# First modulation turned later, input-projection weights in three pairs, filter sums beside their values, one more modulation group in the projection

## The chip, the core and the metric

The kernel runs on one core of one Trainium2 chip. The metric is the device time of one execution in microseconds (us). The core has a matrix engine (TensorE, PE in the profile), a vector engine (VectorE, DVE), a scalar engine (ScalarE, ACT), GpSimd (POOL) and a sync engine (SyncE, SP), which here only issues DMAs. Each engine works through its own list of instructions in the order in which they were written into it; engines wait for each other by semaphores.

## The reference

Two layers of a hybrid backbone over 1024 latent tokens and 256 context tokens, model width 1024, float32 throughout.

```python
for i in range(DEPTH):                                   # layer 0 is even, layer 1 odd and last
    sh1, sc1, g1, sh2, sc2, g2 = ada_mod(c, ada_w[i], ada_b[i])          # silu(c) @ w + b, six groups of 1024
    u_lat = modulate(rms_norm(h_lat, norm1_g[i]), sh1, sc1)              # h*(1+scale)+shift
    u_ctx = modulate(rms_norm(h_ctx, norm1_g[i]), csh1, csc1)            # same with the context's condition
    if even: y = u @ w_in -> first 512 channels: 2-D FFT groups; other 1536: short conv, Hyena long conv; @ w_out
    else:    y_lat = neighbourhood attention (latent rows, all context keys) @ w_out
    h = h + g1 * y
    h = h + g2 * swiglu(modulate(rms_norm(h, norm2_g[i]), sh2, sc2), w_gate, w_up, w_down)
return rms_norm(h_lat, final_g)
```

The long convolution of layer 0 is done in the frequency domain. Its filters come from a small sine MLP over time; each filter is normalised over time: `h = h / sum(|h|)`. A "modulation" is one group of 1024 columns of `ada_mod`, for both conditions (latent and context); layer 0 has six, numbered m = 0 to 5 (0 shift, 1 scale, 2 gate of the first half, 3 to 5 the same of the second).

## The kernel before, in words

Products are done with operands cut in two: `split` writes a rounded high part (`wh`, ACT cast, line 349) and a low part (`wl`, DVE subtraction, line 351), and a product is three matmuls: high by high, low by high, high by low (`mm`, line 345). Loads are issued by SP (`ld`, line 330) or by POOL (`ldr`, line 336). Tiles come from pools: `S4` (1024 floats a partition), `S2`, `G`, `T` (512), and `W(tag)` for weights with rings by tag: `wh` and `wl` have two places each, `ws`, the staging of a weight before its split, four. A new tile of a ring waits until the tile that held its place is no longer used, and what stands behind it in the same engine's list waits with it.

The work is written by Python generators. `run` draws from them in turns, and that order, placed once more by a scheduler when the program is built, sets each engine's list. Latent tokens are two pieces of 512 columns, context is one of 256. The stages of layer 0 and their places in the profiled execution:

- start (to about 115 us): row norms of `x` and `ctx` (`first_norm`), the filters' MLP (`filter_mlp`), and the first two modulations (`ada_first`: m = 1, then m = 0). `ada_first` loads eight blocks of 128 rows of weight per modulation through POOL into S4, forms two PSUM rows of 2x512, copies them on ACT (line 505), turns them into columns by eight small matmuls, and adds the bias on DVE (lines 512, 515). `first_norm` then turns the normed rows and applies the columns.
- `in_proj` (about 115 to 540 us): 16 blocks of 128 output columns of `w_in`; for each, `weights` loads 128x1024 into `ws` and splits it into a `wh`/`wl` pair, 72 matmuls follow. Block i then draws from fillers by a count per block: `long` (for both orders o: `filter_raw` makes the filter values, `spectrum_l` their spectrum by DFT matmuls), `filt` (the same for the context length, `spectrum_c`), `ada` (modulation groups, below), and `four` and `conv` of the context. From block 4 a block ends in `short_conv` (ACT line 1009, DVE lines 1010 to 1013).
- the latent long convolution with `inverse_last` (to about 780 us), the output projection `out_proj` (evictions on DVE at line 1657, squares for the second norm at lines 577 and 582, the second norm and its transforms by `wino_first`, lines 1724 to 1727; to about 882 us), and the SwiGLU. Layer 1 is the rest, 882 to 2990 us.

`filter_sum("l", o, raw)` forms sum |h|: for four blocks of values, two absolute values on ACT, a maximum and an addition on DVE (lines 780, 782), then ten small matmuls with ones. `spectrum_l` starts it and draws from it in the last two of its four classes.

`ada_group(l, m, conds, where)` makes later modulations on DVE alone: for each of eight column blocks it multiplies a weight tile with the broadcast condition and sums (line 552), four half-tiles per step; `late_groups(ms)` runs several. In `in_proj` the group is m = 2; m = 3 and 4 are drawn in `inverse_last` and `out_proj`.

Of the kernel before, what the change touches and what calls it, by code (L numbers as in the profile page):

```python
# [258 lines left out]
class Builder:  # L259
    def __init__(self, ctx, tc, a, out, taps=None, stop=None):  # L260
# [15 lines left out]
        self.mj = 0  # L276
# [86 lines left out]
    def pair3(self):  # L363

        self.p3 = (getattr(self, "p3", 0) + 1) % 4
# [121 lines left out]
    def ada_first(self):  # L487
# [6 lines left out]
        for m in (1, 0):  # L494
            ps = [self.PP(), self.PP()]
            for kb in range(KB):
                w = self.S4()
                self.ldr(w, a["ada_k"][m, kb])
                for j in (0, 1):
                    self.mm(ps[j][0:2, :], cond[:, 2 * kb:2 * kb + 2], w[:, j * 512:(j + 1) * 512], kb == 0, kb == KB - 1)  # L500
                yield
            col = self.PS()
            for j in (0, 1):
                row = self.G()
                nc.scalar.copy(row[0:2, :], ps[j][0:2, :])
# [21 lines left out]
    def ada_group(self, l, m, conds, where):  # L527
# [13 lines left out]
        ready = [load(m * 8)] if where == "s2" else []  # L541
        for nb in range(m * 8, m * 8 + 8):
            if where != "s2" or nb < m * 8 + 7:
                ready.append(load(nb + len(ready)))
# [17 lines left out]
    def late_groups(self, ms):  # L562

        self.load_cond(wide=False)
        for m in ms:
            yield from self.ada_group(0, m, (0, 1), "s2")
# [314 lines left out]
    def spectrum_l(self, o, raw):  # L881
# [4 lines left out]
        tot = self.filter_sum("l", o, raw)  # L886
# [59 lines left out]
        for i in classes:  # L946
            cls, eo = i % 2, i // 2
            kept = []
            for p in (0, 1):
# [3 lines left out]
                for k in (0, 1):  # L953
# [41 lines left out]
        for _ in tot:  # L995
            pass
# [19 lines left out]
    def in_proj(self, u, norm, fill, four, conv):  # L1016
# [16 lines left out]
        def filled(i):  # L1033
# [3 lines left out]
            if i > 4:  # L1037
# [14 lines left out]
        pairs = [self.weights(a["w_in"][nb]) for nb in (0, 1)]  # L1052
# [20 lines left out]
        for i, nb in enumerate(order[2:], 2):  # L1073
            wh, wl = self.weights(a["w_in"][nb])
# [1352 lines left out]
    def run(self):  # L2427
# [24 lines left out]
        for _ in range(4):  # L2452
# [4 lines left out]
        long = (x for o in (0, 1) for g in (self.filter_raw("l", raws["l"], (o,)), self.spectrum_l(o, raws["l"][o]))  # L2457
                for x in g)
        ada = self.late_groups((2,))
# [17 lines left out]
        self.in_proj(u, ng, ((long, (4, 4, 4, 4, 4, 4, 5, 5, 1)), (filt, (0,) * 7 + (2,)), (ada, (0,) * 8 + (1,))), fc, cc)  # L2477
# [5 lines left out]
        late = self.late_groups((3, 4))  # L2483
# [286 lines left out]
```

## Time and profile before

| what | value |
|---|---|
| median of three runs | 2985.84 us (2981.18 to 2989.96) |
| the profiled execution | 2991.98 us, its span 2990.1 us |
| mean granted TensorE clock of it | 0.968 |
| PE busy | 2808.6 us, 94% of the span |
| DVE, ACT, POOL busy | 2069.3, 1328.2, 542.7 us |
| PE busy, start 0 to 115 us | 82.69 of 115 us |
| PE busy, `in_proj` 115 to 540 us | 349.76 of 425 us |
| PE busy, 540 to 780 us | 221.59 of 240 us |
| PE busy, output projection 780 to 882 us | 91.84 of 102 us |
| PE busy, 882 to 2990 us | 2062.70 of 2108 us |

In lines of the profile L349 is line 349 of the kernel, `x4` a count, and a bracket at the end of a line is the engine's idle time just before the work and what ended it: `[7.88 <-DVE s L782]` is 7.88 us of waiting for an `s` tile that DVE wrote at line 782. A float32 matmul is two records. In a table of windows each engine's busy time stands with its count of instructions, then the granted clock, the share of the DMA engines and GB/s.

### The profile page before, as it was taken

How to read it: one execution, taken by the hardware profiler on the slowest of the kernel's cores; microseconds unless marked ns; L12 is line 12 of the kernel's file. 1: busy time of each engine (PE TensorE's matmuls, PEld its weight loads, DVE VectorE, ACT ScalarE, POOL GpSimd, SP SyncE). 2: the span in 40 equal slices, each digit the busy share in tenths (PEclk: the TensorE clock that was granted, in tenths of full speed). 3: DMA queues.
4: the chain of work that ended last, by engine and by line, in shares of the span. 5: the costliest groups of instructions: out<-in, count | busy, mean ns of one | idle time of the engine just before them, and what ended most of it. 6: DMA issues, size and time to landing. Idle time of an engine off the chain costs nothing. (4 is left out here: it accounts for less than half of the span.)

```text
span 2990.1 us, 43785 instructions
## 1 busy us (share of the span) xinstructions
PE 2808.6 (94%) x15570; PEld 2349.1 (79%) x15570; DVE 2069.3 (69%) x3643; ACT 1328.2 (44%) x2274; POOL 542.7 (18%) x867
## 2 busy tenths in 40 slices
PE   5888769989989999999999999999999999999998
PEld 1767558768879888888888988888887788888886
DVE  2575758777787688887678535777777987664545
ACT  3342422543355433333346434777765533333433
POOL 1021113523101122222110001323321022112000
PEclk8889879999999999999999999999999999999999
DMA  6135424666556555656897434778776276534663
GB/s 251 63 131 159 150 76 143 200 219 219 183 192 197 190 198 195 206 208 239 308 313 245 157 129 127 183 184 190 195 224 208 101 248 222 176 110 172 223 196 127
DMA packets 301673, 557.36 MB, mean 186 GB/s; under 512 B 82440, under 2 KB 128714, under 8 KB 301454
## 3 DMA queue, kind: packets, MB, share of 16 engines
q1 hardware_dynamic: 239502, 371.53, 39.8%
q0 software_dynamic: 59648, 178.83, 17.1%
q10 hardware_dynamic: 2304, 4.20, 0.4%
q8 instruction: 123, 2.02, 0.3%
q14 instruction: 96, 0.79, 0.1%
HBM read 407.10 MB, written 119.80 MB: 176 GB/s over the span
## 5 line engine op out<-in xcount | busy, mean ns | idle before, releaser
L1850 PE MATMUL ps<-s,s 128*128 128x512 f32 x1976 | 489.1, 390 | 1.6 <-ACT g L1855 1.6
L1850 PEld LDWEIGHTS ps<-s,s 128*128 128x128 f32 x1976 | 371.8, 188 | 80.1 <-ACT g L1855 2.5
L345 PE MATMUL ps<-s,wh 128*128 128x256 f32 (+1 forms) x1768 | 410.6, 336 | 18.7 <-ACT wh L349 10.0
L345 PEld LDWEIGHTS ps<-s,wh 128*128 128x128 f32 x1768 | 303.9, 196 | 54.4 <-ACT wh L349 10.6
L351 DVE TENSOR_TENSOR wl<-ws,wh 128x1024 fp32r<-128x1024 f32 (+1 forms) x141 | 167.9, 1191 | 181.9 <-ACT wh L349 179.0
L349 ACT CAST wh<-ws 128x1024 fp32r<-128x1024 f32 (+1 forms) x141 | 144.6, 1025 | 303.5 <-PE ps L345 194.9
L345 PE MATMUL ps<-s,wl 128*128 128x256 f32 (+1 forms) x884 | 272.2, 334 | 0.8 <-DVE wl L351 0.8
L345 PE MATMUL pq<-s,wh 128*128 128x512 f32 (+1 forms) x856 | 261.4, 385 | 4.0 <-DVE s L2596 2.6
L2023 PE MATMUL ps<-s,s 128*128 128x512 f32 (+1 forms) x1000 | 259.5, 383 | 3.1 <-DVE s L351 3.0
L349 ACT CAST s<-s 128x1024 fp32r<-128x1024 f32 (+2 forms) x192 | 172.4, 926 | 191.6 <-DMA s<-d 165.8
L345 PE MATMUL ps<-s,s 128*128 128x65 f16 (+4 forms) x2737 | 232.1, 238 | 21.8 <-ACT s L349 7.0
L349 ACT CAST s<-t 128x512 fp32r<-128x512 f32 (+2 forms) x238 | 134.3, 581 | 216.6 <-PE ps L1850 70.6
L351 DVE TENSOR_TENSOR s<-s,s 128x1024 fp32r<-128x1024 f32 (+2 forms) x170 | 190.9, 1154 | 50.5 <-ACT s L349 50.3
L2023 PEld LDWEIGHTS ps<-s,s 128*128 128x128 f32 x1000 | 184.6, 188 | 41.0 <-DVE s L351 4.4
L351 DVE TENSOR_TENSOR s<-t,s 128x512 fp32r<-128x512 f32 (+2 forms) x238 | 151.6, 651 | 68.4 <-ACT s L349 41.2
L1850 PE MATMUL ps<-s,wh 128*128 128x512 f32 x616 | 191.2, 390 | 0.0
L345 PEld LDWEIGHTS ps<-s,wl 128*128 128x128 f32 x884 | 170.1, 195 | 17.6 <-DVE wl L351 1.2
L345 PEld LDWEIGHTS pq<-s,wh 128*128 128x128 f32 x856 | 155.9, 191 | 32.2 <-DVE s L2596 2.7
L345 PE MATMUL pq<-s,wl 128*128 128x512 f32 (+1 forms) x428 | 163.0, 384 | 0.0
L345 PEld LDWEIGHTS ps<-s,s 128*128 128x128 f32 (+1 forms) x817 | 126.6, 195 | 34.2 <-ACT s L349 8.0
L2023 PE MATMUL ps<-s 128*128 128x512 f32 (+1 forms) x500 | 150.7, 385 | 0.0
L336 POOL DMA_DIRECT2D d<-s x154 | 83.4, 542 | 360.2 <-DVE s L1657 120.1
(479 smaller groups left out, 5588.5 us busy)
## 6 DMA issues: line engine op xcount, KB each, us to landing
s<-d SPq DMA_DIRECT2D x283, 256.0 KB, 3.8
s<-in_down SPq DMA_DIRECT2D x150, 256.0 KB, 4.2
d<-s POOLq DMA_DIRECT2D x138, 256.0 KB, 3.4
s<-in_ada_w POOLq DMA_DIRECT2D x56, 512.0 KB, 4.8
d<-tk POOLq DMA_DIRECT2D x98, 256.0 KB, 4.1
ws<-in_up SPq DMA_DIRECT2D x44, 512.0 KB, 3.8
d<-g POOLq DMA_DIRECT2D x86, 256.0 KB, 3.1
ws<-in_gate SPq DMA_DIRECT2D x42, 512.0 KB, 3.7
```

The costliest lines, as they stand in the source:

```text
L336: self.last_ldr = self.nc.gpsimd.dma_start(out, in_).ins
L345: self.nc.tensor.matmul(o, l, r, start=st, stop=sp)
L349: self.last_hi = nc.scalar.copy(hi, src).ins
L351: self.last_lo = eng.tensor_tensor(lo, src, hi.bitcast(F32), SUB).ins
L1850: nc.tensor.matmul(ps, x[:, sl], y, start=first and j == 0 and x is wh and y is xh, stop=j == 3 and x is wl, skip_group_check=True)
L2023: m = nc.tensor.matmul(acc[j][:, c0:c1], x[:, sl], y[:, xs], start=first and k == 0, stop=last and k == 2, skip_group_check=True)
```

## The change

Four things change.

1. `ada_first`: the columns of m = 1 are no longer turned when its rows are done but while m = 0 is under way (at its fifth block), and the row copies go to DVE.
2. `in_proj` takes its weights by `weights3`: every third pair goes into two places of the `ws` ring, the others into `wh` and `wl` as before. The counter `p3`, which a later stage (the SwiGLU of `pair3`) also uses, starts at 0 once, so that stage begins at another place of its own cycle.
3. `filter_sum("l")` is drawn beside `filter_raw`, at its steps k = 3, 5, 7 and so on; what is left of it, the small matmuls among it, is drawn at one place of `spectrum_l`.
4. Modulation m = 3 moves from the later stages into `in_proj`: `ada` takes (2, 3) and is drawn once a block from block 3 and twice from block 13; only m = 4 stays for later. Its weight tiles go as one load of 512 KB into the `ws` ring, where two loads of 256 KB went into S2. `long` is drawn 4 times a block and 2 from block 8, and `four` starts at block 8 where it was block 5.

```diff
-            if where == "s2":
-                st = [self.S2(), self.S2()]
-                for j in (0, 1):
-                    self.ld(st[j], a["ada_w"][l, nb, :, j * 512:(j + 1) * 512])
-                return st
+            if where == "ws":
+                t = self.W("ws", "ws")
+                self.ld(t, a["ada_w"][l, nb])
+                return [t[:, :512], t[:, 512:]]
...
+    def weights3(self, src):
+
+        self.p3 = (self.p3 + 1) % 3
+        st = self.W("ws", "ws")
+        tags = ("ws", "ws") if self.p3 == 0 else ("wh", "wl")
+        hi, lo = self.pair2(tags)
+        self.ld(st, src)
+        self.split(st, hi, lo)
+        return hi, lo
...
-        for m in (1, 0):
-            ps = [self.PP(), self.PP()]
-            for kb in range(KB):
-                w = self.S4()
-                self.ldr(w, a["ada_k"][m, kb])
-                for j in (0, 1):
-                    self.mm(ps[j][0:2, :], cond[:, 2 * kb:2 * kb + 2], w[:, j * 512:(j + 1) * 512], kb == 0, kb == KB - 1)
-                yield
+
+        def columns(m, ps):
             col = self.PS()
             for j in (0, 1):
                 row = self.G()
-                nc.scalar.copy(row[0:2, :], ps[j][0:2, :])
+                nc.vector.tensor_copy(row[0:2, :], ps[j][0:2, :])
...
+        ps = {}
+        for m in (1, 0):
+            ps[m] = [self.PP(), self.PP()]
+            for kb in range(KB):
+                w = self.S4()
+                self.ldr(w, a["ada_k"][m, kb])
+                for j in (0, 1):
+                    self.mm(ps[m][j][0:2, :], cond[:, 2 * kb:2 * kb + 2], w[:, j * 512:(j + 1) * 512], kb == 0, kb == KB - 1)
+                if m == 0 and kb == 4:
+                    columns(1, ps[1])
+                yield
+        columns(0, ps[0])
...
-    def spectrum_l(self, o, raw):
+    def spectrum_l(self, o, raw, tot):
...
-        tot = self.filter_sum("l", o, raw)
...
-                    if i >= 2:
-                        next(tot, None)
-                        if i == 3 and p == 0:
-                            for _ in tot:
-                                pass
+                    if i == 2 and p == 0 and k == 1:
+                        for _ in tot:
+                            pass
...
-            if i > 4:
+            if i > 7:
                 next(four, None)
...
-            wh, wl = self.weights(a["w_in"][nb])
+            wh, wl = self.weights3(a["w_in"][nb])
...
+        def filters():
+            for o in (0, 1):
+                tot = self.filter_sum("l", o, raws["l"][o])
+                for k, _ in enumerate(self.filter_raw("l", raws["l"], (o,))):
+                    if k > 2 and k % 2:
+                        next(tot)
+                    yield
+                yield from self.spectrum_l(o, raws["l"][o], tot)
+
+        long = filters()
+        ada = self.late_groups((2, 3))
...
-        self.in_proj(u, ng, ((long, (4, 4, 4, 4, 4, 4, 5, 5, 1)), (filt, (0,) * 7 + (2,)), (ada, (0,) * 8 + (1,))), fc, cc)
+        self.in_proj(u, ng, ((long, (4, 4, 4, 4, 4, 4, 4, 4, 2)), (filt, (0,) * 7 + (2,)), (ada, (0, 0, 0) + (1,) * 10 + (2,))), fc, cc)
...
-        late = self.late_groups((3, 4))
+        late = self.late_groups((4,))
```

How this moves instructions is shown at three places; in these rows the name before the arrow is written, those behind it are read, and the number behind a name tells tiles apart. Line numbers of the changed kernel are up to 20 higher than those of the kernel before.

First DVE's list in the start stage, around the end of the filters' MLP. Before:

```order
L701 TENSOR_SCALAR s_51_176<-s_51_176 128x640
L703 SCALAR_TENSOR_TENSOR s_48_169<-s_51_176,s_48_169 128x640 x3
L704 TENSOR_SCALAR s_48_169<-s_48_169 128x640
L715 TENSOR_TENSOR s_52_184<-s_48_169,s_52_184 64x512
L717 TENSOR_TENSOR s_53_185<-s_48_169,s_53_185 64x512
L715 TENSOR_TENSOR s_54_190<-s_48_169,s_54_190 64x128
L717 TENSOR_TENSOR s_55_191<-s_48_169,s_55_191 64x128
L512 TENSOR_TENSOR c_97<-ps_218,c_101 128x8
```

and in the changed kernel:

```order
L717 TENSOR_SCALAR s_51_176<-s_51_176 128x640
L351 TENSOR_TENSOR wl_961<-ws_959,wh_960 128x1024
L719 SCALAR_TENSOR_TENSOR s_48_169<-s_51_176,s_48_169 128x640 x3
L720 TENSOR_SCALAR s_48_169<-s_48_169 128x640
L731 TENSOR_TENSOR s_52_184<-s_48_169,s_52_184 64x512
L733 TENSOR_TENSOR s_53_185<-s_48_169,s_53_185 64x512
L731 TENSOR_TENSOR s_54_190<-s_48_169,s_54_190 64x128
L733 TENSOR_TENSOR s_55_191<-s_48_169,s_55_191 64x128
L509 COPY g_241<-ps_151 2x512
L509 COPY g_247<-ps_152 2x512
```

The split of a third weight pair, `wl_961`, now stands inside the MLP, and the two row copies behind its last line; PE's small matmuls that turn m = 1 read `g_241` and `g_247`, and PE's list has the first two matmuls of m = 0 ahead of them now.

Second DVE's list near the end of `in_proj`, where the weights of block 14 (counted from 0) are split. Before, the low half (`wl_4005`) is made ahead of the short convolution of block 13 (its lines 1010 follow it):

```order
L826 COPY t_3771<-s_956_3625 128x512
L1097 TENSOR_TENSOR s_966_3648<-t_3649 128x256
L1098 TENSOR_TENSOR s_966_3648<-t_3649 128x256
L827 TENSOR_TENSOR t_3771<-s_956_3625,s_958_3630 1x512
L828 TENSOR_SCALAR t_3771<-t_3771 1x512
L351 TENSOR_TENSOR wl_4005<-ws_4003,wh_4004 128x1024
L1010 SCALAR_TENSOR_TENSOR s_976_3741<-ps_3666,c_317,s_976_3741 128x255
L1010 SCALAR_TENSOR_TENSOR s_977_3745<-ps_3667,c_317,s_977_3745 128x511
```

and in the changed kernel, where block 14 is one of the third pairs, it (`wl_3845`) stands behind that short convolution and behind two modulation steps (line 568 is the line 552 of before):

```order
L568 ISA ws_3796,ah_3813<-ws_3796,s_470_1584,c_101 128x512
L568 ISA ah_3813 128x1
L1105 TENSOR_TENSOR t_3833<-s_991_3758,s_992_3762 128x512
L850 SCALAR_TENSOR_TENSOR t_3942<-s_995_3773,c_95,t_3784 128x512
L1544 TENSOR_TENSOR s_1015_3816<-ps_3631,t_3817 128x2x64
L1547 TENSOR_TENSOR s_1015_3816<-ps_3631,t_3817 128x63
L1548 TENSOR_TENSOR s_1015_3816<-ps_3631,t_3817 128x64
L568 ISA ws_3796,c_97<-ws_3796,s_471_1585,ah_3813 128x512
L568 ISA c_97 128x1
L1108 TENSOR_TENSOR s_1018_3832<-t_3833 128x256
L1109 TENSOR_TENSOR s_1018_3832<-t_3833 128x256
L351 TENSOR_TENSOR wl_3845<-ws_3843,wh_3844 128x1024
```

From the first of the short convolution's lines that can only run when block 13's matmuls are done, 38 rows of DVE stand ahead of this split, 16 of them (eight pairs) of modulation steps.

Third DVE's list at the end of the output projection, its evictions (line 1657, 1668 in the changed kernel) and the second norm's transforms. Before:

```order
L1724 SCALAR_TENSOR_TENSOR s_1825_7291<-s_1649_6370,c_97,t_7041 128x512
L1724 SCALAR_TENSOR_TENSOR s_1832_7331<-s_1651_6376,c_97,t_7041 128x512
L1724 SCALAR_TENSOR_TENSOR s_1836_7365<-s_1649_6370,c_97,t_7041 128x512
L1657 SCALAR_TENSOR_TENSOR s_1787_7087<-ps_7222,c_97,s_1787_7087 128x512
L582 TENSOR_TENSOR tk_7129<-tk_7129,tk_7168 128x512
L1657 SCALAR_TENSOR_TENSOR s_1788_7089<-ps_7262,c_97,s_1788_7089 128x512
L1657 SCALAR_TENSOR_TENSOR s_1789_7091<-ps_7302,c_97,s_1789_7091 128x512
L1727 SCALAR_TENSOR_TENSOR s_1798_7133<-s_1797_7131,c_97,s_1798_7133 128x512
L1727 SCALAR_TENSOR_TENSOR s_1805_7173<-s_1804_7171,c_97,s_1805_7173 128x512
```

and in the changed kernel:

```order
L1668 SCALAR_TENSOR_TENSOR s_1763_7039<-ps_7174,c_97,s_1763_7039 128x512
L598 TENSOR_TENSOR tk_7081<-tk_7081,tk_7120 128x512
L351 TENSOR_TENSOR wl_7170<-ws_7168,wh_7169 128x1024
L1735 SCALAR_TENSOR_TENSOR s_1794_7203<-s_1674_6421,c_97,t_6993 128x512
L1738 SCALAR_TENSOR_TENSOR s_1774_7085<-s_1773_7083,c_97,s_1774_7085 128x512
L1738 SCALAR_TENSOR_TENSOR s_1781_7125<-s_1780_7123,c_97,s_1781_7125 128x512
L598 TENSOR_TENSOR tk_7081<-tk_7081,tk_7160 128x512
L1738 SCALAR_TENSOR_TENSOR s_1788_7165<-s_1787_7163,c_97,s_1788_7165 128x512
L1668 SCALAR_TENSOR_TENSOR s_1764_7041<-ps_7214,c_97,s_1764_7041 128x512
L351 TENSOR_TENSOR wl_7210<-ws_7208,wh_7209 128x1024
```

Before, seven transforms of one kind and then seven of the other stand in a clump between evictions; now they are spread, one to three between two evictions. No modulation step is left in this stage's list: m = 4 takes the places that m = 3 had in `inverse_last`, and the eight steps of m = 4 that stood in the first half of `out_proj` are gone from it.

More of the change, by code (lines that the diff above doesn't have):

```diff
@@ L275, in __init__ @@
         self.k = self.mk = self.pk = 0
-        self.mj = 0
+        self.mj = self.p3 = 0
         self.held = False
@@ L363, in pair3 @@
     def pair3(self):
-        self.p3 = (getattr(self, "p3", 0) + 1) % 4
+        self.p3 = (self.p3 + 1) % 4
         tags = ("ws", "ws") if self.p3 % 2 == 0 else ("wh", "wl")
@@ L539, in load @@
             return [t[:, :512], t[:, 512:]]
-        ready = [load(m * 8)] if where == "s2" else []
+        ready = [load(m * 8)] if where == "ws" else []
         for nb in range(m * 8, m * 8 + 8):
-            if where != "s2" or nb < m * 8 + 7:
+            if where != "ws" or nb < m * 8 + 7:
                 ready.append(load(nb + len(ready)))
@@ L565, in late_groups @@
         for m in ms:
-            yield from self.ada_group(0, m, (0, 1), "s2")
+            yield from self.ada_group(0, m, (0, 1), "ws")
     def ada_col(self, l, pc, m, b):
@@ L994, in spectrum_l @@
                 yield
-        for _ in tot:
-            pass
     def short_conv(self, acc, hb):
@@ L1050, in kept @@
             return t
-        pairs = [self.weights(a["w_in"][nb]) for nb in (0, 1)]
+        pairs = [self.weights3(a["w_in"][nb]) for nb in (0, 1)]
         p01 = [{}, {}]
@@ L2456, in run @@
         next(ng)
-        long = (x for o in (0, 1) for g in (self.filter_raw("l", raws["l"], (o,)), self.spectrum_l(o, raws["l"][o]))
-                for x in g)
-        ada = self.late_groups((2,))
+        def filters():
[8 more added lines that the diff above has]
+        ada = self.late_groups((2, 3))
         filt = (x for o in (0, 1) for g in (self.filter_raw("c", raws["c"], (o,)), self.spectrum_c(o, raws["c"][o]))
```

## The prediction

> **What bounds the kernel now.** I read the page first: the span, the shares of the engines, and PE's slices.
>
> ```profile
> span 2990.1 us, 43785 instructions
> PE 2808.6 (94%) x15570; PEld 2349.1 (79%) x15570; DVE 2069.3 (69%) x3643; ACT 1328.2 (44%) x2274; POOL 542.7 (18%) x867
> PE   5888769989989999999999999999999999999998
> PEclk8889879999999999999999999999999999999999
> ```
>
> PE is the bound, and what it lacks lies in the first seven slices of 75 us; the change touches nothing behind 882 us. So only PE's idle time up to there can be won. The windows by stage give how much that is, and how full DVE is at the places that the change moves work to and from.
>
> ```profile
> core 0: us, PE busy (x) PEld busy (x) DVE busy (x) ACT busy (x) POOL busy (x), PEclk, DMA share, GB/s
> 0.00:115.00 115.00, 82.69 (x328) 46.58 (x328) 43.43 (x78) 50.24 (x82) 14.75 (x33) 0.90 0.46 166
> 115.00:540.00 425.00, 349.76 (x1646) 281.03 (x1647) 275.54 (x575) 138.43 (x266) 76.84 (x105) 0.88 0.41 132
> 780.00:882.00 102.00, 91.84 (x452) 77.67 (x451) 77.79 (x154) 42.09 (x68) 8.64 (x17) 0.93 0.58 204
> ...
> 380.00:400.00 20.00, 4.26 (x20) 3.08 (x18) 17.11 (x45) 9.39 (x18) 1.57 (x3) 0.68 0.30 92
> 460.00:480.00 20.00, 20.00 (x107) 17.13 (x106) 19.41 (x39) 4.09 (x6) 8.09 (x7) 1.00 0.60 196
> 480.00:500.00 20.00, 20.00 (x101) 16.86 (x100) 16.52 (x33) 6.57 (x12) 4.60 (x5) 1.00 0.36 119
> 500.00:520.00 20.00, 17.88 (x91) 15.03 (x91) 19.78 (x41) 7.42 (x13) 7.11 (x9) 0.83 0.56 165
> 840.00:860.00 20.00, 16.29 (x63) 12.64 (x63) 18.66 (x34) 14.36 (x24) 3.08 (x6) 0.91 0.60 213
> 860.00:880.00 20.00, 13.55 (x64) 12.10 (x62) 16.24 (x23) 10.04 (x15) 1.23 (x3) 0.74 0.52 182
> ```
>
> PE is idle for 75.2 us of `in_proj`, 32.3 of the start and 10.2 of the output projection. DVE is free for a third of `in_proj` as a whole, but from 460 to 520 it is busy for 55.7 of 60 us: modulation steps put there have no room.
>
> Then the waits up to 420 us, and PE's own rows at the stalls.
>
> ```profile
> ACT wh L349 <- PE ps L345: 72.7, 9, 18.4
> DVE wl L351 <- ACT wh L349: 58.9, 9, 10.5
> PE ps L345 <- DVE s L782: 12.0, 2, 7.9
> ```
>
> ```profile
> 190.85 0.55 PE L345 MATMUL ps<-c,s 128*128 128x1 f32 x2 [7.88 <-DVE s L782]
> ...
> 256.77 0.50 PE L345 MATMUL ps<-s,s 128*128 128x512 f32 x1 [3.60 <-ACT s L349]
> ...
> 323.37 0.56 PE L345 MATMUL ps<-c,s 128*128 128x1 f32 x2 [4.17 <-DVE s L782]
> ...
> 401.98 0.59 PE L345 MATMUL ps<-s,c 128*2 128x512 f32 x1 [17.42 <-ACT s L349]
> ...
> 432.29 2.93 PE L345 MATMUL pq<-s,tk 128*128 128x512 f32 x6 [5.51 <-ACT s L981]
> ```
>
> ACT stands 72.7 us in front of a weight's high half until the pair two blocks back is released, and DVE behind it; everything else in their lists (filter values, spectra) stands behind that. This is what three pairs loosen. The filter sums hold PE for 12.0 us, and the largest stall, 17.42 us, is a spectrum's operand that ACT cast after a DVE that was busy for 17.11 of 20 us.
>
> **Start.**
>
> ```profile
> 51.83 1.05 ACT L505 COPY g<-ps 2x512 f32<-2x512 f32 x2
> ...
> 52.31 0.29 DVE L717 TENSOR_TENSOR s<-s,s 64x128 fp32r<-64x128 f32 x1
> 52.52 1.77 PEld L345 LDWEIGHTS ps<-c,g 2*128 2x128 f32 x8 [18.04 <-issue]
> 52.55 1.83 PE L345 MATMUL ps<-c,g 2*128 2x2 f32 x8 [17.14 <-ACT g L505]
> 54.31 3.57 PE L345 MATMUL ps<-s,c 128*2 128x512 f32 x4
> ...
> 60.05 12.18 PE L345 MATMUL ps<-s,c 128*2 128x512 f32 x28
> ```
>
> PE waits 17.14 us for the ACT copy, which came behind the MLP's casts. Now the copies stand on DVE behind the MLP's last line (52.31 + 0.29 = 52.60) and behind one split more. Two DVE rows give the prices:
>
> ```profile
> L351 DVE TENSOR_TENSOR wl<-ws,wh x32: 1211/1224/1226, 38.5 to 848.1; 128x1024 fp32r<-128x1024 f32 x32
> ...
> 364.57 1.29 DVE L764 TENSOR_TENSOR s<-ps,s 128x512 f32<-128x512 f32 x2 [4.09 <-DMA s<-in_win_c]
> ```
>
> The split is 1.22 us, a DVE read of 512 PSUM columns 0.65; so the turn starts near 52.6 + 1.2 + 0.65 = 54.5, 1.9 us later. Against that the four records of 3.57 us run inside the wait. Net -1.7. The copy itself on DVE is not in the trace; with ACT at 0.52 and DVE at 0.65 it is between 0 and 0.2 us dearer for each of two, and I take 0.2 in all. Bounds: nothing, if the norm's DVE work behind it sets the pace, and -3.5, if the split falls into DVE's own idle time. I take -1.5. The trace also shows cold matmuls: 3.57/4 = 0.89 us a record after the wait against 12.18/28 = 0.435 later. [...]
>
> **`in_proj`.** Four terms.
>
> Filter sums: the maxima and additions are the same count, and only their place moves.
>
> ```profile
> L782 DVE TENSOR_TENSOR s<-s,t x12: 681/686/689, 169.1 to 324.3; 128x512 f32<-128x512 f32 x12
> ...
> L780 DVE TENSOR_TENSOR t<-t,t x12: 681/684/687, 166.6 to 321.9; 128x512 f32<-128x512 f32 x12
> ```
>
> With four more of the second kind in another form, that is 28 rows of 0.685 us, 9.6 us for each filter. Beside the values they find a DVE that waits (for weights and loads), but the small matmuls are also drawn earlier, and their last addition is in DVE's list not far ahead of them. I keep about 5 us of the 12.0: -7. Bounds: -12 (all gone) and +3 (the values come later by the sums between them).
>
> The stall at 401.98: DVE was full there with a modulation step and the spectra of filter 1. The counts of `long` spread that work over blocks up to 11 and the modulation steps go on, so about 11 of the 17.4 us stay: -6. Bounds -14 and 0.
>
> The releases: the short stalls by ACT casts behind a blocked high half (256.77 is one; 3 to 6 us each). Half of three such: -5. Bounds: -30 (all stalls of `in_proj` that are left) and 0.
>
> What is added: a modulation group.
>
> ```profile
> L552 DVE DVE_READ_ACCUMULATOR2_ANT ah<- x48: 70/82/89, 371.1 to 836.8; 128x1 f32 x48
> ...
> L552 DVE CUSTOM_DVE_ANT_0 t<-s,s,c x24: 730/746/1775, 370.4 to 834.1; 128x512 f32<-128x512 f32 x24
> ```
>
> A step is four pairs: 4 x (0.746 + 0.082) = 3.3 us, a group eight steps, 26.5 us. Five of the eight added steps fall on blocks 3 to 7, where DVE has room, and cost nothing as long as it does. The other three make blocks 13 to 15 carry two each, where the windows above show no room. At block 14 this meets the third pair: its split stands behind 38 rows that start when block 13 ends, 16 of modulation (8 x 0.828 = 6.6 us) and 22 others, most of them of 0.65 to 0.75 us, about 14 us. PE has some 4 us of other matmuls meanwhile: a stall of about 16 us, where before there were some 2 (17.88 of 20 in the window). Net +14. Bounds: 0, if the split's rows run earlier than I count, and +30, if block 15 meets the same.
>
> Sum: -7 - 6 - 5 + 14 = -4. The queues: SP's 32 loads of 256 KB become 16 of 512 KB in `ws` places that a third pair may hold for a block; weights and stores stand behind them on SP. A block of matmuls lies between, so I cost it at nothing; without that cover each such wait would be some us of PE. POOL's loads in the start are the same in the same order. `four` begins later, with three of its steps after the stage, on a PE that is full: nothing.
>
> **Output projection.**
>
> ```profile
> 850.93 0.93 PE L345 MATMUL ps<-s,wh 128*128 128x512 f32 x2 [3.71 <-DVE s L1657]
> ...
> 865.31 0.63 ACT L577 ACTIVATE tk<-s 128x512 f32<-128x512 f32 x1 [5.92 <-DVE tk L582]
> ...
> 870.11 0.80 PE L345 MATMUL ps<-s,wh 128*128 128x256 f32 x2 [6.45 <-ACT wh L349]
> ```
>
> Both stalls are DVE late: PE waits 3.71 us for a PSUM bank to be evicted, then 6.45 for weights that ACT splits only after its squares, which wait 5.92 us for DVE. DVE is late because the modulation steps of m = 4 (26.5 us) stand in the first half of this stage. They go; DVE then has 26 us in hand and its evictions follow PE. Of 3.71 + 6.45 = 10.2 us I take 2 to 3 as left, the last eviction, square and sum having to follow the last matmul in any case. -8. Bounds -13 (the clock of 0.91 and 0.74 there rises too: 29.8 us of PE at 0.83 mean would be some 3 us shorter) and -2.
>
> **The rest.** `inverse_last` has one group on the same places as before; in the SwiGLU the two rings of `pair3` change their turn. 0, with 2 either way.
>
> Sum: -1.5 - 4 - 8 = -13.5. The profiled execution of 2991.98 us becomes 2978.5; it lies 6.1 above the median, and from the median 2985.84 it is 2972.
>
> **The rivals.**
>
> DVE becomes the bound of the last blocks (slower). Place: blocks 13 to 15. For it: 55.7 of 60 us busy there already, two steps a block, a split behind them. Against it: only block 14 is a third pair. Price: if blocks 13 and 15 lose 12 us each as well, in_proj goes to +20, the sum to +10.5: 2996. It decides from about one more such stall on.
>
> The releases bring more (faster still). For it: 72.7 us of ACT waiting ahead of everything; with three pairs nearly all other stalls of `in_proj` could shrink, say by a further 15 of the 75: 2957. Against it: DMA and PE results, not ACT, end many of them.
>
> It doesn't do what it says: the start's gain is eaten by the norm behind it, the sums' stalls only move, and the end of the output projection is set by the chain of last eviction, square and sum. Then -1, 2985. For it: the last stall before 882 does end in a chain. Against it: the 5.92 us that ACT waits for DVE there.
>
> **How the numbers follow.** The forecast as it stands, 2972 (its own range 2963 to 2977): 0.45. The releases bring more: 0.17. Nothing: 0.20. Slower: 0.18. 0.3% is 9 us, about what a measurement of this kernel tells from no change. So faster 0.62, within 0.20, slower 0.18. The range of 8 in 10 runs from the faster rival with 24 us of releases instead of 15 (2948) to just beyond the slower rival's price (2998).
>
> **What would show it.** Right: in the changed profile no modulation line and no stall over 4 us between 840 and 880 us, clock near 1 there; the stalls by the sums' additions together near 5 us; the one large stall of `in_proj` at block 14, released by the low half of a third pair, 12 to 18 us. Wrong: several stalls of that kind at blocks 13 to 15 (the slower rival); a weight load in `ws` landing late, with SP waiting for a matmul; or the stall at 870 unchanged.

## The result and the profile after

The changed kernel takes 2996.05 us (median of nine runs, 2991.48 to 3006.84) against 2986.78 for the kernel before (nine runs, 2981.18 to 2992.04): 1.004 times as long, 95% interval 1.0024 to 1.0055. It is 9 us slower. Forecast were 2972 and a chance of 0.62 for faster. That the time lies in the range is luck: the range reached so far only for the slower rival (2998), whose mechanism did not come.

The execution profiled here took 3006.84 us, 11 above its median, where the one of before was 6 above its own; of the 15 us between the two spans some 5 belong to the executions and not to the kernels. First the page of the changed kernel.

```profile
span 3005.1 us, 43741 instructions
PE 2815.7 (94%) x15570; PEld 2351.6 (78%) x15570; DVE 2079.0 (69%) x3647; ACT 1327.0 (44%) x2270; POOL 540.6 (18%) x867
PEclk8889898999999999999999999999999999999999
```

PE has the same 15570 matmul records, is busy for 7 us more and idle for 8 us more. The windows by stage, and three that the prediction looked at (columns as before):

```profile
0.00:115.00 115.00, 81.88 (x328) 46.97 (x328) 46.70 (x82) 48.47 (x78) 14.40 (x33) 0.88 0.44 162
115.00:540.00 425.00, 349.47 (x1600) 279.52 (x1601) 289.90 (x615) 130.83 (x246) 75.34 (x105) 0.87 0.43 137
540.00:780.00 240.00, 206.33 (x1078) 174.11 (x1078) 187.71 (x322) 107.41 (x164) 85.34 (x79) 0.94 0.62 205
780.00:882.00 102.00, 102.00 (x530) 86.70 (x529) 58.52 (x94) 38.95 (x64) 12.46 (x23) 1.00 0.48 169
...
480.00:500.00 20.00, 7.50 (x43) 6.51 (x42) 14.29 (x29) 5.58 (x9) 4.43 (x4) 0.73 0.15 53
...
840.00:860.00 20.00, 20.00 (x94) 16.36 (x93) 11.36 (x24) 11.11 (x22) 0.16 (x1) 1.00 0.53 167
860.00:880.00 20.00, 20.00 (x90) 16.57 (x89) 19.75 (x29) 11.10 (x16) 3.24 (x6) 1.00 0.82 322
```

The output projection became what was forecast: PE without a gap (102.00 of 102 us busy) and at a granted clock of 1.00 from 780 to 882. But PE has done less by then: 1600 records in the window of `in_proj` where it did 1646, and 1078 from 540 to 780 us where it did 1181. The first matmul behind `in_proj` (line 1210, 1221 now) starts at 539.8 us where it was 528.8, and the first of the output projection (line 1683, 1694 now) at 768.2 where it was 742.1: 11 us are lost up to the first place and 15 more up to the second. PE's rows at four of its stalls:

```profile
53.86 1.83 PE L345 MATMUL ps<-c,g 2*128 2x2 f32 x8 [18.87 <-DVE g L509]
...
170.97 0.56 PE L345 MATMUL ps<-c,s 128*128 128x1 f32 x2 [8.47 <-DVE s L798]
...
498.83 1.01 PE L345 MATMUL ps<-s,wh 128*128 128x256 f32 x2 [12.50 <-ACT wh L349]
...
768.23 2.08 PE L1694 MATMUL ps<-s,wh 128*128 128x256 f32 x5 [5.21 <-ACT wh L349]
```

The stall of block 14 is there (12.50 us), but what ended it is the high half on ACT, not the low half on DVE. Some of ACT's and DVE's rows ahead of it:

```profile
485.07 1.24 ACT L1020 ACTIVATE s<-pq,c 128x256 f32<-128x256 f32 x2 [14.85 <-PE pq L345]
...
497.73 1.04 ACT L349 CAST wh<-ws 128x1024 fp32r<-128x1024 f32 x1 [5.28 <-DVE c L568]
```

```profile
494.75 1.81 DVE L568 CUSTOM_DVE_ANT_0 t<-ws,s,c 128x512 f32<-128x512 f32 x1
496.50 0.07 DVE L568 DVE_READ_ACCUMULATOR2_ANT ah<- 128x1 f32 x1
496.50 1.19 DVE L568 CUSTOM_DVE_ANT_0 ws<-ws,s,ah 128x512 f32<-128x512 f32 x1
497.63 0.07 DVE L568 DVE_READ_ACCUMULATOR2_ANT c<- 128x1 f32 x1
```

The cast does not wait for its data, which SP had issued 32 us earlier (at 465.25; the core's DMA engines moved nothing from 484 to 498 us). What ends its wait is a modulation step of DVE (line 568). That fits a wait for a place to write to: as a third pair its high half goes into the `ws` ring, and the place still holds a modulation tile that DVE has not finished (`v_ws5` below bears this out). The same ring delays loads. SP's waits for modulation steps in the changed kernel, for 115 to 550 us and for 640 to 800 us (before they were 3.4 and 1.5 us):

```profile
SPq L330 <- DVE c L568: 41.4, 8, 11.6
...
SPq L330 <- DVE c L568: 31.7, 5, 17.0
```

and in SP's list the loads of the output projection's weights, first before, then after:

```profile
696.72 0.38 SPq L330 DMA_DIRECT2D ws<-in_w_out  x1
...
717.65 0.90 SPq L330 DMA_DIRECT2D s<-in_ada_w  x2
```

```profile
716.45 9.83 SPq L330 DMA_DIRECT2D ws<-in_ada_w  x4
761.32 1.61 SPq L330 DMA_DIRECT2D ws<-in_w_out  x3
```

Before, the first of these weights is loaded 45 us ahead of its use at 742.1 us and the modulation tiles go elsewhere. After, modulation tiles fill the ring, and the weights are asked for 7 us ahead of the matmuls at 768.23, which wait 5.21 us for their high half.

### The profile page after: what moved, and what is told of

Its sections match the earlier page's. It is cut to its first block, busy times and chain, and to the rows that moved or that the text cites. A ratio compares the mean times of both kernels' runs of the same rounds, so it can differ in the third digit from the quotient of the medians.

```text
span 3005.1 us, 43741 instructions
## 1 busy us (share of the span) xinstructions
PE 2815.7 (94%) x15570; PEld 2351.6 (78%) x15570; DVE 2079.0 (69%) x3647; ACT 1327.0 (44%) x2270; POOL 540.6 (18%) x867
## 5 line engine op out<-in xcount | busy, mean ns | idle before, releaser
L1861 PEld LDWEIGHTS ps<-s,s 128*128 128x128 f32 x1976 | 370.6, 188 | 82.2 <-DVE s L351 2.6
L345 PE MATMUL ps<-s,wh 128*128 128x256 f32 (+1 forms) x1656 | 385.3, 335 | 20.4 <-ACT wh L349 13.9
L345 PEld LDWEIGHTS ps<-s,wh 128*128 128x128 f32 x1656 | 284.2, 195 | 54.6 <-ACT wh L349 14.3
L345 PE MATMUL pq<-s,wh 128*128 128x512 f32 (+1 forms) x968 | 294.1, 381 | 6.8 <-DVE s L2616 3.7
L345 PE MATMUL ps<-s,wl 128*128 128x256 f32 (+1 forms) x828 | 252.5, 331 | 1.0 <-DVE wl L351 0.8
L349 ACT CAST wh<-ws 128x1024 fp32r<-128x1024 f32 (+1 forms) x141 | 144.4, 1025 | 230.7 <-PE ps L345 87.2
L2034 PEld LDWEIGHTS ps<-s,s 128*128 128x128 f32 x1000 | 184.4, 188 | 41.9 <-DVE s L351 5.5
L345 PEld LDWEIGHTS pq<-s,wh 128*128 128x128 f32 x968 | 176.5, 191 | 37.8 <-DVE s L2616 4.5
L345 PE MATMUL pq<-s,wl 128*128 128x512 f32 (+1 forms) x484 | 181.6, 380 | 1.1 <-DVE wl L351 1.1
L345 PEld LDWEIGHTS ps<-s,wl 128*128 128x128 f32 x828 | 157.5, 193 | 18.0 <-DVE wl L351 2.4
L345 PEld LDWEIGHTS ps<-s,s 128*128 128x128 f32 x845 | 130.3, 194 | 37.4 <-ACT s L349 7.3
```

Of the source, the lines that this page charges most:

```text
L345: self.nc.tensor.matmul(o, l, r, start=st, stop=sp)
L349: self.last_hi = nc.scalar.copy(hi, src).ins
L1861: nc.tensor.matmul(ps, x[:, sl], y, start=first and j == 0 and x is wh and y is xh, stop=j == 3 and x is wl, skip_group_check=True)
L2034: m = nc.tensor.matmul(acc[j][:, c0:c1], x[:, sl], y[:, xs], start=first and k == 0, stop=last and k == 2, skip_group_check=True)
```

## The experiments

Each is a small edit, on the changed kernel unless said otherwise; ratios are to the kernel before on the same chip, with 95% intervals. The kernels of the third table ran on another chip than those of the first two, those of the fourth on yet another, so that across tables the ratios are what is compared. The changed kernel itself is at 1.004 (1.0024 to 1.0055). Each build also lets the scheduler place all lists anew, so what an edit costs or brings holds with the order that comes of it.

### One part undone

The added group taken back (`u_group`):

```diff
-        ada = self.late_groups((2, 3))
+        ada = self.late_groups((2,))
...
-(ada, (0, 0, 0) + (1,) * 10 + (2,))
+(ada, (0,) * 8 + (1,))
...
-        late = self.late_groups((4,))
+        late = self.late_groups((3, 4))
```

> The changed kernel with the added modulation group taken back: m = 2 alone in the input projection, once a block from block 8, m = 3 and 4 later as before; weight tiles still in ws. Theory A (the doubled steps and the ws places that their tiles hold delay block 14): the 12.5 us stall at block 14 goes, PE idle of the input projection falls by 10 to 15 us, the output projection takes its 10 us of stalls back; time 2986 to 2992. Theory B (the third pairs delay themselves, whatever the group does): the stall of about 12 us stays and the 10 us come back; 3004 to 3008.

Two pairs again (`u_weights`; the same at the first two blocks):

```diff
-            wh, wl = self.weights3(a["w_in"][nb])
+            wh, wl = self.weights(a["w_in"][nb])
...
```

> The changed kernel with two weight pairs again instead of three. Theory A: block 14 no longer needs two ws places, its 12.5 us stall goes, while ACT's waits for the release of a pair come back (about 70 us of ACT, little of it on PE's path); 2985 to 2992. Theory B (third pairs help the rest of the stage by 10 us or more): 2998 to 3006.

The first modulation as before, copies on ACT (`u_start`): the function `ada_first` of the kernel before.

> The changed kernel with the first modulation turned as before and copied on ACT. The start stage ended 0.3 us later after the change, so both theories expect the same time within 2 us: 2994 to 2998, PE's wait near 52 us back to about 17.1 us.

The sums inside the spectrum, with the old counts of `long` (`u_sums`; the lines in `spectrum_l` that go back as well are left out here):

```diff
-                for k, _ in enumerate(self.filter_raw("l", raws["l"], (o,))):
-                    if k > 2 and k % 2:
-                        next(tot)
-                    yield
+                yield from self.filter_raw("l", raws["l"], (o,))
...
-(long, (4, 4, 4, 4, 4, 4, 4, 4, 2))
+(long, (4, 4, 4, 4, 4, 4, 5, 5, 1))
```

> The changed kernel with the filter sums drawn inside the spectrum again and the counts of the long filters as before (4, 4, 4, 4, 4, 4, 5, 5, 1). The sums' two waits come back to about 12 us from 8.5. Theory A: 2995 to 3002, the stall at block 14 unchanged. Theory C (the early sums and the slower counts push the rest of the filters later, and that is the loss): 2986 to 2991.

| kernel | median us | ratio to before | interval |
|---|---|---|---|
| `u_group` | 2979.04 | 0.9983 | 0.997 to 0.9995 |
| `u_weights` | 2984.16 | 0.9997 | 0.9985 to 1.0009 |
| `u_start` | 3000.46 | 1.0044 | 1.003 to 1.0058 |
| `u_sums` | 3001.52 | 1.0051 | 1.0033 to 1.0068 |

Start and sums make no difference that can be told from the changed kernel; `u_start` lies 2 us above its expected range, and PE's wait near 53 us did not go back to 17.1 (20.96). Undoing either the group or the third pairs takes away the loss against the kernel before, the first by 17 us, the second by 13, and with either the stall of block 14 goes (3.86 us and none over 1.2 there). So this loss needs both parts, and that speaks for what they share, the `ws` ring. But `u_group` is 7 us faster than theory A allowed (`u_weights` 1 us), so theory A is not the whole. And without the third pairs SP still waits for the tiles; its row in `u_weights` for 115 to 550 us:

```profile
SPq L330 <- DVE c L568: 109.4, 14, 19.8
```

### The ring

The groups' tiles in S2 again, by two loads, nothing else undone (`v_s2`), and the same without the added group (`v_group_s2`):

```diff
-            if where == "ws":
-                t = self.W("ws", "ws")
-                self.ld(t, a["ada_w"][l, nb])
-                return [t[:, :512], t[:, 512:]]
+            if where == "s2":
+                st = [self.S2(), self.S2()]
+                for j in (0, 1):
+                    self.ld(st[j], a["ada_w"][l, nb, :, j * 512:(j + 1) * 512])
+                return st
...
```

> The changed kernel with the groups' weight tiles in S2 again, two loads of 256 KB each, and nothing else undone. Theory A1 (a third pair waits for ws places that the groups' tiles hold until DVE has used them): the 12.5 us stall at block 14 shrinks to 4 us or less, as without the group; 2982 to 2988. Theory A2 (DVE's doubled steps alone make the split late, wherever the tile lies): the stall stays over 8 us; 2994 to 3000.

> The kernel without the added group, and the tiles of all groups in S2 as before: what is left of the change is the start, the three pairs, the sums and the counts of long and four. If the ws ring also costs in the later stages (the kernel without the group lost 14 us between 540 and 770 us, where group 3 and 4 now load into ws beside the output projection's weights), the loss there shrinks by 5 to 10 us and the time is 2968 to 2975; if it does not, 2977 to 2981.

Five places in the ring, two fewer in S2 (`v_ws5`):

```diff
-        self.p2 = ent(tc.tile_pool(name="p2", bufs=35))
+        self.p2 = ent(tc.tile_pool(name="p2", bufs=33))
...
-bufs=4 if tag == "ws" else 2)
+bufs=5 if tag == "ws" else 2)
```

> The changed kernel with five places in the ws ring instead of four, and two fewer in S2 to make room. The kernel's order of DVE keeps block 14's split behind block 13's short convolution and the two steps. Theory A1: the ring is what counts, the stall falls under 6 us; 2983 to 2990. Theory A2: the stall stays over 8 us, since the split's place in DVE's list stays; 2993 to 2999.

One modulation step in every block (`v_spread`): the counts of `ada` are `(1,)`.

> The changed kernel with one modulation step in each of the 16 blocks instead of none in three and two in three. Theory A2: without doubled steps the stall at block 14 falls to 4 to 8 us; 2985 to 2992. Theory A1: one step a block still holds a ws place and the stall stays near 12 us; 2994 to 2999.

| kernel | median us | ratio to before | interval |
|---|---|---|---|
| `v_s2` | 2966.43 | 0.9947 | 0.9933 to 0.996 |
| `v_group_s2` | 2965.19 | 0.9939 | 0.9927 to 0.9951 |
| `v_ws5` | 2997.57 | 1.0052 | 1.0039 to 1.0065 |
| `v_spread` | 3004.77 | 1.0077 | 1.0063 to 1.0092 |

The place of the tiles is the loss, and more: with them in S2 the changed kernel is 16 us faster than before, about 28 us faster than as it was made, and also 16 us faster than theory A1 expected. (The edit changes the size of the loads with the place; the size alone was not tried. The kernel before with large loads into `ws`, below, is not slower.) The windows of `in_proj` and of 540 to 780 us of `v_s2`, and SP's first load of the output projection's weights:

```profile
115.00:540.00 425.00, 361.00 (x1701) 291.97 (x1702) 305.58 (x650) 143.48 (x271) 81.38 (x109) 0.90 0.47 150
540.00:780.00 240.00, 223.63 (x1205) 191.74 (x1204) 183.99 (x314) 104.37 (x153) 85.07 (x85) 0.95 0.61 205
...
686.05 0.38 SPq L330 DMA_DIRECT2D ws<-in_w_out  x1
```

101 records more fit into the window of `in_proj` than after the change, 127 more into the next, and the first of the output projection's weights is loaded at 686 us (696 before). The stall at block 14 is gone (no wait over 3.3 us between 400 and 515 us). The pair of block 14 is split at 406.4 us (high half) and 429.5 (low half), 91 and 74 us earlier than in the changed kernel: with the place free, the new order has the low half ahead of the rows of DVE that the prediction counted, too.

`v_ws5` meets theory A1 in the stall and theory A2 in the time. The stall fell to 5.01 us and is now ended by the low half, so a fifth place does free the cast (it runs at 459.7 us, where it was 497.73):

```profile
497.12 1.01 PE L345 MATMUL ps<-s,wl 128*128 128x256 f32 x2 [5.01 <-DVE wl L351]
```

and the first layer ended earlier: the SwiGLU's products at line 1861, whose first of one form starts at 1015.5 us in the trace of the changed kernel, start at 997.8 (1004.9 in the kernel before). The total is no better; in its trace the 7 us ahead of the kernel before are given back in the second layer, and it is 3 us behind at 2975. Two S2 tiles are missing there, but `v_s2`, which has them all, gives back 7 us too; why was not tried. `v_spread` parts stall and time as well. Block 14 waits only 3.86 us there, as theory A2 had it, but the steps now in the first blocks bring stalls of 9.39 and 6.10 us at 133 and 155 us, and the total grew beyond both expected ranges. So the stall of block 14 goes or falls to 5 us in any of five ways (no group, no third pairs, no doubled steps, a fifth place, tiles elsewhere), and it was only 12.5 us of the 28. What separates the kernels with tiles in S2 is how little SP waits for modulation steps: in `v_s2` 9.4 us from 115 to 550 and 0.4 from 640 to 800, against 41.4 and 31.7, and no cast of a weight waits for one.

### Is it the ring alone, and what gains once it is free?

The kernel before with nothing changed but its tiles in `ws` (`x_before_ws`): the diff of `v_s2`, the other way.

> The kernel before, with one thing changed: the weight tiles of the modulation groups go as one load of 512 KB into the ws ring. Theory A1, that the shared ring costs by itself (without the added group it cost 14 us, 2979 against 2965): 2992 to 3000, SP waiting for modulation lines of DVE, and the output projection starting 5 to 12 us later. Rival, that it costs only where a third pair takes two more places: 2982 to 2987.

On `v_s2`, two pairs (`x_s2_pairs2`, the diff of `u_weights`, with `p3` starting at 1), the old start (`x_s2_start`), the old sums and counts of `long` (`x_s2_sums`):

> The changed kernel with the groups' tiles in S2, and two weight pairs instead of three (the counter set so that the SwiGLU's rings turn as in the changed kernel). If the third pairs are what gains once the ring is free: 2976 to 2986. If they gain nothing: 2964 to 2969.

> The changed kernel with the groups' tiles in S2, and the first modulation as before. The start stage ended as early before as after, so 2964 to 2970; if the later turn was worth the 1.5 us that the prediction gave it, 2967 to 2970, which a run of this kernel hardly tells from none.

> The changed kernel with the groups' tiles in S2, the filter sums inside the spectrum again and the counts of the long filters as before. The sums' waits would go from about 5 us to 10 to 12: 2970 to 2976. If the values beside the filters gain nothing: 2964 to 2969.

| kernel | median us | ratio to before | interval |
|---|---|---|---|
| `x_before_ws` | 2984.17 | 0.9992 | 0.9982 to 1.0002 |
| `x_s2_pairs2` | 2959.11 | 0.9911 | 0.9896 to 0.9926 |
| `x_s2_start` | 2963.43 | 0.9929 | 0.9913 to 0.9945 |
| `x_s2_sums` | 2956.79 | 0.9905 | 0.989 to 0.992 |

In the kernel before the ring may be shared without a net cost; theory A1 fails there. But this is a sum of two things. In the trace of `x_before_ws` `in_proj` ended 20 us earlier (first matmul behind it at 509.2, 528.8 before), with the stall of 17.42 us down to 10.74, and 13 us of that are lost again up to the output projection (735.1 against 742.1), whose first weights are late too (issued at 726.98, a wait of 8.28 us at 735). This trace is the fastest of its twelve executions, 10 us under their median, so the sizes are rough.

What the tiles in `ws` cost instead of S2 is different in each kernel: nothing here, 13 us with third pairs and one group in `in_proj` (`u_group` against `v_group_s2`, 0.9983 against 0.9939), about 25 us with two groups and two pairs (`u_weights` against `x_s2_pairs2`, 0.9997 against 0.9911; some 3 of it the rings' turn, below), about 28 with all of it. So the rival in that expectation, third pairs alone, doesn't hold either: two groups are enough. These kernels differ from the kernel before in `four`, the sums and the start as well, so that the price goes by the number of tiles is not shown.

And with the ring free neither the third pairs nor the early sums gain: both kernels without them are under both of their expected ranges, and their intervals do not overlap with that of `v_s2`. That is 11 and 13 us by ratios of two chips; against `x_s2_start`, from the same chip, it is 4 and 7 us, and the intervals overlap. Nor do the traces put it in the stage that was changed: the first SwiGLU products start at 974.7 us in `v_s2`, 976.3 in `x_s2_pairs2` and 971.3 in `x_s2_sums`, the last records of line 2023 (2035, 2035 and 2037 there), near the end of the second layer, at 2952.3, 2949.1 and 2945.1. So 4 to 5 us come in the second layer, which none of these edits touches (the order there differs between `v_s2` and `x_s2_pairs2` from 2320 us on). So no gain by these parts is shown, and no loss by them either. Start: no difference shown.

### What does gain

Four kernels made from the kernel before. `four` from block 8 (`y_four`):

```diff
-            if i > 4:
+            if i > 7:
                 next(four, None)
```

> The kernel before with one change: `four` starts at block 8 where it was block 5. Theory F (the gain in the input projection is the later start: the stall of 17.4 us at 402 us stood behind rows of `four` on DVE): the stall falls under 8 us and the time to 2970 to 2978. Rival (it only moves work): 2983 to 2988.

The group moved, tiles in S2, and the counter of the SwiGLU's rings as after the change (`y_group`); with `four` from block 8 as well (`y_group_four`); the counter alone (`y_parity`):

> The kernel before with the group m = 3 moved into the input projection at the changed kernel's counts, its tiles in S2, and the SwiGLU's rings turning as in the changed kernel. Theory F: the input projection loses 5 to 15 us by DVE, the output projection gains 10 and the SwiGLU 4: 2978 to 2987. Rival G (the moved group is the gain): 2962 to 2972.

> The two together on the kernel before: the group moved with tiles in S2, the rings' turn, and `four` from block 8. If start, third pairs and early sums all gain nothing, this equals the best so far: 2953 to 2960. If they gain together what they don't singly: 2962 to 2972.

> The kernel before with the counter of the SwiGLU's rings starting at 1, nothing else. The wait of 3.57 us at 994.7 us that all kernels with the old turn show goes: 2980 to 2982. If it is an accident of other shifts: 2984 to 2987.

| kernel | median us | ratio to before | interval |
|---|---|---|---|
| `y_four` | 2980.87 | 0.9987 | 0.9977 to 0.9998 |
| `y_group` | 2988.19 | 1.0013 | 1.0003 to 1.0023 |
| `y_group_four` | 2958.98 | 0.9915 | 0.9903 to 0.9928 |
| `y_parity` | 2981.5 | 0.9991 | 0.9981 to 1.0 |

Neither the moved group nor the later `four` is worth much alone (+4, -4 us), together they are worth 25. (`y_four` lies between its two expected ranges, `y_group` 1 us above that of theory F; `y_group_four` and `y_parity` are within theirs.) `y_group_four` has neither the early sums, the third pairs, the turned start nor the `ws` tiles, and its interval overlaps with that of the best here. The windows of `in_proj` in `y_group` and in `y_group_four`:

```profile
115.00:540.00 425.00, 351.67 (x1620) 282.66 (x1620) 290.55 (x623) 131.37 (x250) 73.79 (x104) 0.87 0.43 135
```

```profile
115.00:540.00 425.00, 361.66 (x1729) 294.10 (x1730) 308.07 (x652) 144.97 (x273) 86.28 (x110) 0.91 0.48 151
```

The second gets 109 more PE records done at a clock of 0.91 against 0.87. The traces say where the two need each other. The first matmul behind `in_proj` starts at 528.8 us before, 514.0 in `y_four`, 537.4 in `y_group` and 506.1 in `y_group_four`; from the first of the output projection to the first SwiGLU products it takes 262.8 us before, 245.1 in `y_group` and 248.9 in `y_group_four`. So in these traces the moved group gains behind `in_proj` with either `four`, and in `in_proj` it costs time with the early `four` and none with the later. The largest stall of `in_proj` there is 17.42 us before at 401.98, and in `y_four`, `y_group` and `y_group_four`

```profile
373.39 0.98 PE L345 MATMUL pq<-s,s 128*128 128x256 f32 x3 [11.20 <-ACT s L981]
```

```profile
413.55 0.59 PE L345 MATMUL ps<-s,c 128*2 128x512 f32 x1 [10.31 <-ACT s L349]
```

```profile
376.35 0.98 PE L345 MATMUL pq<-s,s 128*128 128x256 f32 x3 [8.06 <-ACT t L789]
```

Theory F, that this stall stood behind `four`, is half right: in `y_four` and `y_group_four` the matmul that waited 17.42 us does not wait any more, but another one in the same stretch waits 11.20 and 8.06 us, and the time fell by 4 us where 7 or more were expected. Why the two need each other is not settled. The filler `four` and the group's steps both draw S2 tiles, and with `four` from block 5 they do so in the same blocks. `x_before_ws` fits this, where the tiles leave S2 and `in_proj` ends early with `four` unmoved; that it is the reason was only argued.

The counter's price, some 3 us, lies at the edge of what the runs tell (0.9981 to 1.0). What it does shows: a wait in the SwiGLU of the first layer, before and in `y_parity`.

```profile
994.72 0.80 PE L345 MATMUL ps<-s,wh 128*128 128x256 f32 x2 [3.57 <-ACT wh L349]
```

```profile
980.97 0.50 PE L345 MATMUL ps<-s,wh 128*128 128x256 f32 x2 [0.86 <-ACT wh L349]
```

## Why the prediction was wrong, point by point

- Start, -1.5. PE's wait was 18.87 us where 19.0 was worked out, but that shows little: in the eight kernels with the old start it lies between 17.14 and 20.96. The copies cost what was taken (0.675 us each on DVE, 0.574 on ACT). The four records run ahead of the wait brought nothing: the turning of the norm behind it ended 0.3 us later than before, and undoing the part changed nothing that can be told. That fits the bound of nothing named there, DVE's norm work setting the pace.
- Filter sums, -7. One of two waits went (4.17), the other grew (7.88 to 8.47), so 12.0 became 8.5. But the first is gone in `u_sums` and `y_four` too, which have the old sums, so the part did not do it. And shorter waits were not time: `x_s2_sums`, where the wait is back at 7.87, is no slower than `v_s2`, where it is 5.29 (0.9905 against 0.9947, with the counts of `long` among it). A gain of 7 was put where none is shown.
- The stall at 401.98, -6. In the changed kernel it is gone from there (no wait above 4.6 us between 330 and 480), more than forecast. The reason given, the counts of `long`, is not the one: `u_sums` has the old counts and no wait above 4 us there either, and in `y_four`, with the old counts, that matmul does not wait any more.
- Releases, -5. ACT's wait for the pair does fall (in the page, from 194.9 us to 87.2 over the kernel), and no gain shows: `x_s2_pairs2`, without third pairs, is no slower. ACT's idle time was not PE's.
- The added group, +14 at block 14. The place and the size were right (12.50), the cause only in part. The prediction counted DVE rows ahead of the low half. The wait is ended by the high half, which waits for a place in the ring that DVE's modulation rows give free at 497.7 us. With a fifth place it falls to 5.01 us, which the low half then ends. What the prediction counted is thus the smaller part, some 5 us.
- The queues, nothing. This is the step that failed: "SP's 32 loads of 256 KB become 16 of 512 KB in `ws` places that a third pair may hold for a block; ... I cost it at nothing." The prediction took a block of matmuls as cover for a tile that waits for a pair's release. The other direction counts: casts of a third pair and loads of later weights wait for tiles that DVE releases late. The tiles' place costs about 28 us (1.004 against 0.9947), and it reached past `in_proj` to the first weights of the output projection. The 28 us hold the stall of block 14, for which the prediction had 14 by another cause. So about 14 of the 23 us between the forecast of -13.5 and the measured 9 are this term's, and some 9 are gains that did not come, an estimate from these figures. That `v_s2` (2966) ends near the forecast is luck as well, as it gets there by other terms.
- Output projection, -8. Right in mechanism and place: both stalls are gone, the clock is at 1.00. From the start of the output projection to the SwiGLU's products at line 1850 (1861 now) its lag on the kernel before falls from 26 to about 11 us in these traces, so the term was rather too small (some 3 us of this are the rings' turn). Its bound has a slip: reckoned as there, with PE's time in proportion to the clock, 29.8 us at a mean of 0.83 (840 to 880 us, before) would be 5 us shorter at 1.00, not 3; that is an estimate from these windows, the proportion itself was not shown, and the forecast does not use it.
- The rest, 0. The lag grew by 15 us between the end of `in_proj` and the output projection, where SP waits for modulation steps and the weights come late; the prediction had looked for a price of the ring only in `in_proj`. The SwiGLU's other turn brought about 3 us (`y_parity`), at the edge of what is told.
- `four` later, "nothing": alone near -4 us, but with the moved group 25 together, the largest gain found in the change.

The slower rival that was written down (blocks 13 to 15 each stalling, 2996) has the right time and the wrong mechanism: only block 14 stalls. Its 0.18 was too little for a case in which one resource is given a second and a third user at once.

The granted clock is lower around the stall of block 14: from 480 to 500 us it is 0.73, with PE busy for 7.50 of 20 us, where before it was 1.00 with PE busy for all 20. Over the window of `in_proj` it is 0.87 against 0.88; PE is idle there for about as long as before (75.5 against 75.2 us) and does 46 records less. How much of that is slower matmuls and how much another mix of work, the windows don't separate.

## What to carry to other kernels

A ring of buffers is a queue between engines: before a new user goes into it, ask for each place who releases it, how late that engine is, and which casts and loads stand behind the wait, also in stages after the one that is changed. Price each part of a change by an experiment of its own before crediting it: here two parts that looked like gains (third pairs, early sums) showed none, one that was costed at nothing (`four` later) carried the gain, and it did so only together with another. A wait that another engine has (ACT's 72.7 us) is no gain until PE is shown to stand behind it.

## What was not expected of the hardware

Two executions of the same instructions differ by some 6 us in one stage. `y_parity` runs the same code as the kernel before up to the SwiGLU; in its trace `in_proj` ends about 6 us earlier, with PE idle for 68.9 us up to 520 where before it was 70.8. From 115 to 520 us before, then `y_parity`:

```profile
115.00:520.00 405.00, 334.18 (x1567) 268.42 (x1568) 266.67 (x559) 127.69 (x246) 76.84 (x105) 0.88 0.41 132
```

```profile
115.00:520.00 405.00, 336.15 (x1594) 269.79 (x1595) 267.26 (x562) 128.10 (x246) 75.68 (x104) 0.89 0.41 132
```

27 records more in nearly the same busy time, an estimated 5.7 us at 0.211 us a record. So a difference of 5 or 6 us between two single traces says nothing here. The prices above go by the runs; the places that traces gave them are sure only where they differ by more.
